# A norm's weights spread by two small matmuls, a first product group cut in two, and a scaling issued later

## The chip, the cores and the metric

The kernel runs on one core of a Trainium2 chip. A core has a matmul engine (TensorE, "PE" in the profile, with its weight loads as "PEld"), a vector engine (VectorE, "DVE"), a scalar engine (ScalarE, "ACT"), GpSimd ("POOL") and SyncE ("SP"), which here issues most of the transfers. The metric is the device time of one execution in microseconds (us); lower is better. Engines run side by side and wait for each other on semaphores. Each engine works through its own instructions in order.

## The reference, cut to what matters

One encoder layer over 2048 tokens of width 1024. Its first step, the only one that the change touches, is an RMS norm of the input and the first products with the mixer's input weights:

```python
def rmsnorm(x, gain):
    x32 = x.astype(jnp.float32)
    y = x32 * lax.rsqrt(jnp.mean(jnp.square(x32), axis=-1, keepdims=True) + EPS)
    return (y * gain.astype(jnp.float32)).astype(x.dtype)

def mlstm_mixer(xn, w_in, b_gates, head_norm, w_out):
    u = xn @ w_in                       # 1024 -> q 512, k 512, v 1024, o 1024, gates 16
    q, k, v, o, g = jnp.split(u, [...])
    ...                                 # forward and backward scan over 16 chunks of 128 tokens
    return h.astype(xn.dtype) @ w_out

h = x
xn = rmsnorm(h, norm_mix[0])
h = h + mlstm_mixer(xn, w_in, b_gates, head_norm, w_out)
h = h + sqrelu_mlp(rmsnorm(h, norm_mlp[0]), mlp_w1, mlp_w2)
...                                     # a gated embedding term and a last norm
```

## The kernel before, in words

All products are made from float32 numbers split into two parts: `hi`, the number rounded to TensorE's reduced float32, and `lo`, the rest. ACT casts the `hi`, DVE subtracts to get the `lo`, and three products (hi by hi, hi by lo, lo by hi) make one full product. So every operand costs a cast on ACT and a subtraction on DVE before PE can use it.

The first stage computes the first 512 columns of v for tokens 1024 to 2047 (block 1), in eight groups of 128 tokens (tiles). Its actors are:

- `p0` and `p1`, two `Prep` objects with four tiles of 128 tokens each. `p0` goes tile by tile, so that products can start early: `dma1(j)` loads tile j (`raw`, 512 KB); `norm1(j)` squares it on ACT (a sum along the row is a by-product), makes the inverse root by a chain of five small DVE and two small ACT operations (`rstd`), and scales it on DVE into `xs`, with the norm's weights as a row in all 128 partitions (`rowc["mix"]`); `tr1(j)` transposes the eight 128x128 blocks of `xs` on PE into two accumulator banks (`pt`), from which four casts on ACT and four subtractions on DVE fill `xT`. `p1` goes by all four tiles at once: `square(j)` four times, `scale()` (one `rstd` and four scalings on DVE), and `tr(k)` for the eight slices k, with the norm's weights per partition (`gains["mix"]`).
- `v0`, a job with four weights of 512 KB (`v0.weights`, each two slices of 128 rows) and eight groups (`v0g`). `prep()` of a weight is one cast on ACT (`whi`) and one subtraction on DVE (`wlo`). A group is 24 matmuls of 512 columns into one accumulator bank (`psv`) and a copy out (`ev`, on DVE for even tiles and on ACT for odd ones). Group 0 has an order of its own: first all 16 products with `whi`, then the 8 with `wlo`.

Three things set the order. Between `strict(V, A, TE)` (L1466) and `strict()` (L1504) the instructions of DVE, ACT and PE are issued on each engine in just the order in which the program text names them. Transfers of SP are issued in the order of the text as far as their buffers are free, and run in that order. After `strict()` the framework itself orders each engine's instructions by the order of the text and by the times that it expects; the last line of the stage, `v0.groups = [lambda: weave(...)]`, hands it tile 3's group together with `p1`'s eight `tr(k)`. Accumulator banks come from a pool of four for products (`ps_mm`) and one of three for transposes (`ps_tr`). In the profile most instructions carry L98 or L100, the lines of the helper that issues them, strict or not; so they are told apart by their tiles.

Of the kernel before, what the change touches and what calls it, by code (L numbers as in the profile page):

```python
# [8 lines left out]
F32 = mybir.dt.float32  # L9
F32R = mybir.dt.float32r  # L10
AF = mybir.ActivationFunctionType
ALU = mybir.AluOpType
# [4 lines left out]
P = 128  # L17
S = 2048
D = 1024
KD = D // P  # L20
# [15 lines left out]
def hybrid_mlstm_kernel(  # L36
# [23 lines left out]
    const = ctx.enter_context(tc.tile_pool(name="const", bufs=1))  # L60
# [4 lines left out]
    def ps_mm(name):  # L65
        return psm.tile([P, 512], F32, tag="mm", bufs=4, name=name)
# [7 lines left out]
    def Ht(name, shape, dt=F32):  # L74

        return sb.tile(shape, dt, tag="H", bufs=NH, name=name)
# [5 lines left out]
    def St(name, shape, dt=F32):  # L82

        return sb.tile(shape, dt, tag="S", bufs=6, name=name)
# [20 lines left out]
    def strict(*engines):  # L105
        for e in (V, A, TE):
            e.strict = e in engines

    V, A, G, TE, SP = Engine(nc.vector), Engine(nc.scalar), nc.gpsimd, Engine(nc.tensor), nc.sync


    rowc = {}
# [22 lines left out]
    ones = const.tile([P, P], F32, name="ones")  # L135
# [3 lines left out]
    def gain_load(nm, g):  # L139
        SP.dma_start(gains[nm], g.rearrange("(k p) -> p k", p=P))  # L140
# [15 lines left out]
    def weave(main, side):  # L156
        n, done = len(main), 0
        for i, f in enumerate(main):
            upto = -(-(i + 1) * len(side) // n)
            for g in side[done:upto]:  # L160
                g()
            done = upto
            f()
# [5 lines left out]
    def rstd(ss, n, out=None):  # L169

        T = lambda nm: sb.tile([P, 8], F32, tag=nm, bufs=3, name=nm)[:, :n]
        a, y, t = T("rsa"), T("rsy"), T("rst")
        V.tensor_scalar_add(a, ss, EPS)
        act(y, a, AF.Ln)
        act(y, y, AF.Exp, scale=-0.5)
        V.tensor_tensor(t, a, y, op=ALU.mult)
        V.tensor_tensor(t, t, y, op=ALU.mult)
        V.tensor_scalar(t, t, -0.5, 1.5, op0=ALU.mult, op1=ALU.add)
        out = y if out is None else out
        V.tensor_tensor(out, y, t, op=ALU.mult)  # L180
        return out

    def small(nm, bufs=3):
        return sb.tile([P, 8], F32, tag=nm, bufs=bufs, name=nm)

    def mm3(ps, lh, ll, rh, rl, first, last, **kw):
        TE.matmul(ps, lh, rh, start=first, stop=False, **kw)
        TE.matmul(ps, lh, rl, start=False, stop=False, **kw)
        TE.matmul(ps, ll, rh, start=False, stop=last, **kw)
# [63 lines left out]
    class Prep:  # L253
# [50 lines left out]
        def norm1(self, j):  # L304
            ss = small("ss1")
            xs = Ht("xs", [P, D])
            A.activation(xs, self.raw[j], AF.Square, scale=1.0 / 32.0, accum_out=ss[:, 0:1])
            r = rstd(ss[:, :1], 1)
            V.scalar_tensor_tensor(xs, self.raw[j], r[:, 0:1], rowc["mix"], op0=ALU.mult, op1=ALU.mult)
            self.xs1 = xs  # L310

        def tr1(self, j):
# [254 lines left out]
    def store(c, dst, src):  # L567
        (SP if c >= 8 else G).dma_start(dst, src)
# [39 lines left out]
    def v_groups(prs, blk, c0, n, ws, nk):  # L608

        gate = c0 + n == D  # L610

        def group(tt):
            def f():
                ps = ps_mm("psv")[:, :n + 16 * gate]
                pr = prs[tt // 4]
                sl = slice((tt % 4) * P, (tt % 4 + 1) * P)
                if blk == 1 and c0 == 0 and tt == 0:

                    for k in range(KD):
                        for xk in (pr.hi, pr.lo):  # L620
                            TE.matmul(ps, xk[k][:, sl], ws[k // nk].hi[:, k % nk], start=k == 0 and xk is pr.hi, stop=False)
                    for k in range(KD):
                        TE.matmul(ps, pr.hi[k][:, sl], ws[k // nk].lo[:, k % nk], start=False, stop=k == KD - 1)
                else:
                    for k in range(KD):
                        w = ws[k // nk]
                        mm3(ps, pr.hi[k][:, sl], pr.lo[k][:, sl], w.hi[:, k % nk], w.lo[:, k % nk],
                            k == 0, k == KD - 1)
                t = St("ev", [P, 512])[:, :n]
                (A.copy if tt % 2 else V.tensor_copy)(t, ps[:, :n])  # L630
                store(blk * 8, pr.rows(v_d, blk * 8 + tt)[..., c0:c0 + n], t)
                if gate:
                    if tt == 0:
                        gt[blk] = sb.tile([P, 8, 16], F32, tag="gt", name="gt")
                    V.tensor_copy(gt[blk][:, tt], ps[:, n:])
            return f
        return [group(tt) for tt in range(8)]

    def w_rows(k0, k1, c0, n):
        return w_in[k0 * P:k1 * P, c0:c0 + n].rearrange("(k p) n -> p k n", p=P)  # L640
# [1 line left out]
    def v_jobs(prs, blk):  # L642
        wa = [Weight(w_rows(k, k + 2, VC, 512), [P, 2, 512]) for k in range(0, KD, 2)]
        wb = [Weight(w_rows(k, k + 4, VC + 512, 256), [P, 4, 256]) for k in range(0, KD, 4)]
        wc = [Weight([w_rows(k, min(k + 3, KD), c0, n) for c0, n in ((VC + 768, 256), (GC, 16))],
                     [P, min(3, KD - k), 272]) for k in range(0, KD, 3)]
        b, c = v_groups(prs, blk, 512, 256, wb, 4), v_groups(prs, blk, 768, 256, wc, 3)
        return Job(v_groups(prs, blk, 0, 512, wa, 2), wa), Job(c + b, wc + wb)

    def gate_rows(blk):  # L650

        pt = ps_tr("ptg")[:, :P]
        TE.transpose(pt, gt[blk].rearrange("p c g -> p (c g)"), ident)
        t = sb.tile([P, P], F32, tag="gr", name="gr")
        V.tensor_copy(t, pt)
        for c in range(8):
            d = g_d[blk * 8:blk * 8 + 8]
            if blk == 1:
                SP.dma_start(d[c], t[c * 16:c * 16 + 16])
            else:  # L660
                q = c % 4
                SP.dma_start(d[c - q:c - q + 4, :, 32 * q:32 * q + 32].rearrange("c g t -> g c t"),
                             t[c * 16:c * 16 + 16].rearrange("g (c t) -> g c t", c=4))
# [776 lines left out]
    def x_tile(t):  # L1440
        return x[t * P:(t + 1) * P, :]

    pa = {1: [Prep(lambda j, s=s: x_tile(8 + s * 4 + j), gains["mix"]) for s in range(2)],
          0: [Early(lambda j, s=s: x_tile(s * 4 + j), gains["mix"], f"mix{s}_d") for s in range(2)]}
# [22 lines left out]
    v0 = jobs[1, "v"][0]  # L1467
    v0.ready = True
    p0 = pa[1][0]
    p0.dma1(0)  # L1470
    rowc["mix"] = Ht("row_mix", [P, D])
    SP.dma_start(rowc["mix"], norm_mix[0].partition_broadcast(P))
    v0.weights[0].dma()
    p0.dma1(1)
    for w in v0.weights[1:]:
# [1 line left out]
    p0.dma1(2)  # L1477
    p0.dma1(3)
    p0.norm1(0)
    v0.weights[0].prep()  # L1480
    p0.tr1(0)
    v0.weights[1].prep()
    v0.weights[2].prep()
    v0.weights[3].prep()
    p0.norm1(1)
    v0g = list(v0.groups)
    v0g[0]()
    p0.tr1(1)
    pa[1][1].dma()
    p0.norm1(2)  # L1490
    p1 = pa[1][1]
    p1.square(0)
    p1.square(1)
    v0g[1]()
    gain_load("mix", norm_mix[0])
    gain_load("hn", head_norm[0])
    p0.tr1(2)
    p0.norm1(3)
    p1.square(2)
    p1.square(3)  # L1500
    p1.scale()
    v0g[2]()
    p0.tr1(3)
    strict()  # L1504
    v0.groups = [lambda: weave(v0g[3:4], pa[1][1].steps()[2:])] + v0g[4:]
    pairs1[0].side.append(lambda: gate_rows(1))
    pairs1[1].side.append(gate_bias)

# [145 lines left out]
    n = ENTER[-1] + NQ  # L1654
# [34 lines left out]
    for t in range(NC):  # L1689
# [12 lines left out]
        g, i = t // 4 + 1, t % 4  # L1702
# [45 lines left out]
```

## Time and profile before

| | |
|---|---|
| Median of 3 runs | 2401.54 us (2399.94 to 2401.57) |
| Span of the profiled execution, first to last instruction | 2396.9 us (no time beside the span is listed for it) |
| PE busy | 2359.8 us, 98% |
| DVE, ACT, POOL busy | 65%, 49%, 26% |
| Mean granted PE clock | 0.997 |

The page lists for each engine its busy time, its share of the span and its number of instructions. "Windows" give the same for stretches of the span. The timeline lists instructions in order of time: start in us, duration in us, engine, line, operation, output <- inputs, shapes, count, and in brackets how long the engine stood idle before it and whom it waited for. The chain of work that ended last is followed back from the last instruction, at each step to what released it.

### The profile page before, as it was taken

How to read it: one execution, taken by the hardware profiler on the slowest of the kernel's cores; microseconds unless marked ns; L12 is line 12 of the kernel's file. 1: busy time of each engine (PE TensorE's matmuls, PEld its weight loads, DVE VectorE, ACT ScalarE, POOL GpSimd, SP SyncE). 2: the span in 40 equal slices, each digit the busy share in tenths (PEclk: the TensorE clock that was granted, in tenths of full speed). 3: DMA queues.
4: the chain of work that ended last, by engine and by line, in shares of the span. 5: the costliest groups of instructions: out<-in, count | busy, mean ns of one | idle time of the engine just before them, and what ended most of it. 6: DMA issues, size and time to landing. Idle time of an engine off the chain costs nothing.

```text
span 2396.9 us, 31578 instructions
## 1 busy us (share of the span) xinstructions
PE 2359.8 (98%) x11221; PEld 1949.9 (81%) x11221; DVE 1564.8 (65%) x2611; ACT 1164.3 (49%) x2166; POOL 629.9 (26%) x679
## 2 busy tenths in 40 slices
PE   7999999999999999999999999999999999999998
PEld 6988888788889887888888888787888888888886
DVE  6677545557778887666685544767666667666665
ACT  5234434437788874343353333444444444455554
POOL 0041122124333324446533332011111111111121
PEclk9999999999999999999999999999999999999999
DMA  5676656868668883456663332568686776796453
GB/s 177 228 225 196 192 144 224 281 220 295 230 227 296 277 269 110 132 169 209 215 228 106 106 114 71 176 134 196 142 189 164 170 170 153 173 216 178 136 138 87
DMA packets 274038, 441.18 MB, mean 184 GB/s; under 512 B 48936, under 2 KB 182440, under 8 KB 273880
## 3 DMA queue, kind: packets, MB, share of 16 engines
q1 hardware_dynamic: 211608, 309.00, 39.3%
q0 software_dynamic: 61984, 129.64, 23.2%
q8 instruction: 88, 1.44, 0.2%
q14 instruction: 70, 0.57, 0.1%
q10 hardware_dynamic: 288, 0.52, 0.1%
HBM read 263.39 MB, written 175.50 MB: 183 GB/s over the span
## 4 chain that ended last, share of the span: by engine, by line
PE 91%; DVE 4%; ACT 2%; issue 1%; DMA 1%; POOL 0%; DVEq 0%; ACTq 0%; SPq 0%; POOLq 0%
PE pa L100 33%; PE pb L100 16%; PE pc L100 8%; PE pg L100 7%; PE psf L100 7%; PE psv L100 7%; PE pso L100 5%; PE pn L100 2%; PE pl L100 2%; PE pu L100 2%; PE pt L100 1%; DVE op L100 1%; PE pS L100 0%; ACT jk L100 0%; DMA wst<-in_mlp_w 0%
## 5 line engine op out<-in xcount | busy, mean ns | idle before, releaser
L100 PE MATMUL pa<-op 128*128 128x512 f32 x3360 | 824.2, 394 | 3.6 <-ACT e L100 2.1
L100 PEld LDWEIGHTS pa<-op 128*128 128x128 f32 x3360 | 629.5, 188 | 155.7 <-ACT e L100 4.4
L100 PE MATMUL pb<-op 128*128 128x512 f32 x1632 | 407.7, 394 | 0.8 <-DVE op L100 0.8
L100 PEld LDWEIGHTS pb<-op 128*128 128x128 f32 x1632 | 306.2, 188 | 73.8 <-DVE op L100 1.1
L100 DVE TENSOR_TENSOR op<-sa,op 128x1024 fp32r<-128x1024 f32 (+2 forms) x176 | 189.1, 1080 | 143.3 <-ACT op L100 109.7
L100 ACT CAST op<-sa 128x1024 fp32r<-128x1024 f32 (+2 forms) x176 | 156.6, 894 | 189.7 <-PE pb L100 98.1
L1297 POOL DMA_DIRECT2D h_d<-o x96 | 94.8, 1033 | 529.9 <-DVE o L100 443.7
L100 ACT COPY e<-pa 128x512 f32<-128x512 f32 x160 | 93.7, 586 | 278.4 <-PE pa L100 277.9
L100 PE MATMUL pc<-op 128*128 128x512 f32 x768 | 191.9, 394 | 0.1
L100 PEld LDWEIGHTS pc<-op 128*128 128x128 f32 x768 | 144.1, 188 | 34.6 <-DVE op L100 0.6
L100 PE MATMUL psv<-whi,xT 128*128 128x272 f32 (+2 forms) x720 | 161.1, 317 | 0.6 <-DVE xT L98 0.6
L100 PE MATMUL psf<-xT,whi 128*128 128x512 f32 x512 | 160.9, 395 | 0.0
L100 ACT CAST op<-wst 128x512 fp32r<-128x512 f32 x112 | 92.5, 834 | 113.9 <-DVE op L100 59.8
L100 DVE TENSOR_TENSOR op<-wst,op 128x512 fp32r<-128x512 f32 x112 | 122.8, 1099 | 30.8 <-ACT op L100 18.5
L467 POOL TENSOR_TENSOR sa<-wst 128x512 f32<-128x512 f32 x32 | 58.8, 1838 | 262.2 <-PE pb L100 167.3
L100 PEld LDWEIGHTS psv<-whi,xT 128*128 128x128 f32 x720 | 118.6, 188 | 9.8 <-DVE xT L98 0.8
L100 PE MATMUL psv<-wlo,xT 128*128 128x272 f32 (+2 forms) x360 | 113.8, 316 | 0.0
L100 PEld LDWEIGHTS psf<-xT,whi 128*128 128x128 f32 x512 | 95.4, 188 | 21.3
L100 DVE TENSOR_TENSOR op<-hst,op 128x384 fp32r<-128x384 f32 (+1 forms) x96 | 65.5, 688 | 64.7 <-ACT op L100 45.1
L100 PE MATMUL pso<-whi,hThi 128*128 128x512 f32 x256 | 102.0, 399 | 2.6 <-ACT nt L100 1.4
L100 PE MATMUL pg<-whi,xTh 128*128 128x512 f32 x256 | 101.4, 397 | 0.0
L100 PE MATMUL psf<-xT,wlo 128*128 128x512 f32 x256 | 100.9, 394 | 0.0
(261 smaller groups left out, 4371.4 us busy)
## 6 DMA issues: line engine op xcount, KB each, us to landing
wst<-in_mlp_w SPq DMA_DIRECT2D x96, 512.0 KB, 5.2
h_d<-o POOLq DMA_DIRECT2D x96, 512.0 KB, 13.4
hid_d<-e SPq DMA_DIRECT2D x128, 256.0 KB, 2.5
hst<-hid_d SPq DMA_DIRECT2D x64, 384.0 KB, 6.8
wst<-in_mlstm_w_in SPq DMA_DIRECT2D x44, 512.0 KB, 5.2
vst<-v_d SPq DMA_DIRECT2D x31, 512.0 KB, 4.7
raw<-in_x SPq DMA_DIRECT2D x16, 512.0 KB, 6.6
kq<-kq_d SPq DMA_DIRECT2D x16, 512.0 KB, 4.0
```

The costliest lines, as they stand in the source:

```text
L100: r = f(*a, **kw)
L467: eng.tensor_tensor(s[:, 0], r1[:, :, P:], r2[:, :, P:], op=add_)
L1297: G.dma_start(rows(h1_d, 2 * q + i), o[i], accum_op=add_)
```

## The change

The norm's weights are loaded as one row of 4 KB (`row1`). Two matmuls with a row of ones spread its halves over 128 partitions in two accumulator banks. The scaling of tile 0 reads those banks in two halves; then ACT copies both halves into a tile in SBUF, which the later tiles use. Group 0 becomes two functions, `high` (16 products) and the rest (8 products and the copy out), with the transpositions of tile 1 between them. The norm of tile 1 goes ahead of the cast of the fourth weight. The scaling of `p1` goes behind the transpositions of tile 3.

```diff
             r = rstd(ss[:, :1], 1)
-            V.scalar_tensor_tensor(xs, self.raw[j], r[:, 0:1], rowc["mix"], op0=ALU.mult, op1=ALU.mult)
+            for g, sl in rowc["mix"]:
+                V.scalar_tensor_tensor(xs[:, sl], self.raw[j][:, sl], r[:, 0:1], g, op0=ALU.mult, op1=ALU.mult)
             self.xs1 = xs
...
         def group(tt):
+            first = blk == 1 and c0 == 0 and tt == 0
+            pr, sl = prs[tt // 4], slice((tt % 4) * P, (tt % 4 + 1) * P)
+            ps1 = []
+
+            def high():
+                ps = ps_mm("psv")[:, :n]
+                ps1.append(ps)
+                for k in range(KD):
+                    for xk in (pr.hi, pr.lo):
+                        TE.matmul(ps, xk[k][:, sl], ws[k // nk].hi[:, k % nk], start=k == 0 and xk is pr.hi, stop=False)
+
             def f():
-                ps = ps_mm("psv")[:, :n + 16 * gate]
-                pr = prs[tt // 4]
-                sl = slice((tt % 4) * P, (tt % 4 + 1) * P)
-                if blk == 1 and c0 == 0 and tt == 0:
-
-                    for k in range(KD):
-                        for xk in (pr.hi, pr.lo):
-                            TE.matmul(ps, xk[k][:, sl], ws[k // nk].hi[:, k % nk], start=k == 0 and xk is pr.hi, stop=False)
+                ps = ps1[0] if first else ps_mm("psv")[:, :n + 16 * gate]
+                if first:
                     for k in range(KD):
                         TE.matmul(ps, pr.hi[k][:, sl], ws[k // nk].lo[:, k % nk], start=False, stop=k == KD - 1)
...
-            return f
-        return [group(tt) for tt in range(8)]
+            return [high, f] if first else [f]
+        return [f for tt in range(8) for f in group(tt)]
...
     p0.dma1(0)
-    rowc["mix"] = Ht("row_mix", [P, D])
-    SP.dma_start(rowc["mix"], norm_mix[0].partition_broadcast(P))
+    row1 = const.tile([1, D], F32, name="row1")
+    SP.dma_start(row1, norm_mix[0].unsqueeze(0))
+    halves = [slice(n * 512, (n + 1) * 512) for n in range(2)]
+    rowc["mix"] = []
+    for sl in halves:
+        pb_ = ps_mm("prow")
+        TE.matmul(pb_, ones[0:1], row1[:, sl], start=True, stop=True)
+        rowc["mix"].append((pb_, sl))
     v0.weights[0].dma()
     p0.dma1(1)
...
     p0.norm1(0)
+    row = Ht("row_mix", [P, D])
+    for pb_, sl in rowc["mix"]:
+        A.copy(row[:, sl], pb_)
+    rowc["mix"] = [(row, slice(0, D))]
     v0.weights[0].prep()
     p0.tr1(0)
     v0.weights[1].prep()
     v0.weights[2].prep()
+    p0.norm1(1)
     v0.weights[3].prep()
-    p0.norm1(1)
     v0g = list(v0.groups)
     v0g[0]()
     p0.tr1(1)
     pa[1][1].dma()
+    v0g[1]()
     p0.norm1(2)
     p1 = pa[1][1]
     p1.square(0)
     p1.square(1)
-    v0g[1]()
+    v0g[2]()
     gain_load("mix", norm_mix[0])
     gain_load("hn", head_norm[0])
     p0.tr1(2)
     p0.norm1(3)
     p1.square(2)
     p1.square(3)
+    v0g[3]()
+    p0.tr1(3)
     p1.scale()
-    v0g[2]()
-    p0.tr1(3)
     strict()
-    v0.groups = [lambda: weave(v0g[3:4], pa[1][1].steps()[2:])] + v0g[4:]
+    v0.groups = [lambda: weave(v0g[4:5], pa[1][1].steps()[2:])] + v0g[5:]
```

## The prediction

> **What bounds the kernel now.** I read the page first: the span, the engines, the chain by engine.
>
> ```profile
> span 2396.9 us, 31578 instructions
> PE 2359.8 (98%) x11221; PEld 1949.9 (81%) x11221; DVE 1564.8 (65%) x2611; ACT 1164.3 (49%) x2166; POOL 629.9 (26%) x679
> PE 91%; DVE 4%; ACT 2%; issue 1%; DMA 1%; POOL 0%; DVEq 0%; ACTq 0%; SPq 0%; POOLq 0%
> ```
>
> The matmul engine (PE) is the bound; only its idle time can be won, 37.1 us in all. The windows by stage say where it lies, and the chain in order of time where the steady run begins.
>
> ```profile
> 0.00:8.60 8.60, 0.00 (x0) 0.00 (x0) 2.17 (x7) 3.41 (x6) 0.83 (x7) 1.00 0.72 252
> 8.60:20.10 11.50, 9.62 (x40) 7.09 (x40) 8.81 (x15) 6.53 (x13) 0.00 (x0) 1.00 1.04 401
> 33.60:45.20 11.60, 9.83 (x55) 7.55 (x56) 11.04 (x19) 6.36 (x12) 0.00 (x0) 1.00 0.25 75
> 45.20:2396.00 2350.80, 2326.95 (x11064) 1924.65 (x11062) 1534.54 (x2546) 1137.04 (x2110) 629.04 (x672) 1.00 0.63 184
> 20.13 5.82 PE psv L98 x24
> 45.11 69.85 PE psv L100 x483
> ```
>
> The second number is the stretch, the third PE's busy time. Before 45.1 us PE stands 8.6 us waiting for data, some 2 us around the first tile and nearly 2 us between 33.6 and 45.2. After 45.1 it runs on. So the change is worth what it moves two moments by: the start of tile 1's products (20.13, call it T1), and the stretch after 33.6. The page gives no time beside the span; the median, 2401.54, is 4.6 us above it, and I carry that 4.6 over.
>
> The timeline of the first tile, all engines, thinned:
>
> ```profile
> 1.28 0.41 SPq L1472 DMA_DIRECT2D row_mix<-in_norm_mix  x1
> 4.61 1.06 ACT L98 ACTIVATE xs<-raw 128x1024 f32<-128x1024 f32 x1 [2.52 <-DMA raw<-in_x]
> 6.21 0.20 ACT L98 ACTIVATE rsy<-rsy 128x1 f32<-128x1 f32 x1
> 7.21 1.28 DVE L98 SCALAR_TENSOR_TENSOR xs<-raw,rsy,row_mix 128x1024 f32<-128x1024 f32 x1
> 8.03 1.05 ACT L98 CAST whi<-wst 128x1024 fp32r<-128x1024 f32 x1 [1.61 <-DMA wst<-in_mlstm_w_in]
> 8.88 1.70 PE L98 MATMUL pt<-ident,xs 128*128 128x128 f32 x7
> 9.11 1.23 DVE L98 TENSOR_TENSOR wlo<-wst,whi 128x1024 fp32r<-128x1024 f32 x1 [0.61 <-ACT whi L98]
> 9.77 0.37 ACT L98 CAST xT<-pt 128x256 fp32r<-128x256 f32 x1 [0.69 <-PE pt L98]
> 10.24 2.00 PE L98 MATMUL psv<-whi,xT 128*128 128x512 f32 x4
> 10.25 0.42 DVE L98 TENSOR_TENSOR xT<-pt,xT 128x256 fp32r<-128x256 f32 x1
> 11.48 0.37 ACT L98 CAST xT<-pt 128x256 fp32r<-128x256 f32 x1 [0.21 <-DVE xT L98]
> 11.75 2.94 ACT L98 CAST whi<-wst 128x1024 fp32r<-128x1024 f32 x3
> 12.83 3.50 DVE L98 TENSOR_TENSOR wlo<-wst,whi 128x1024 fp32r<-128x1024 f32 x3 [0.52 <-ACT whi L98]
> 14.60 1.06 ACT L98 ACTIVATE xs<-raw 128x1024 f32<-128x1024 f32 x1
> 15.78 2.01 PE L98 MATMUL psv<-wlo,xT 128*128 128x512 f32 x8
> 16.24 0.15 DVE L98 TENSOR_SCALAR rsa<-ss 128x1 f32<-128x1 f32 x1
> 17.66 1.29 DVE L98 SCALAR_TENSOR_TENSOR xs<-raw,rsy,row_mix 128x1024 f32<-128x1024 f32 x1
> 19.01 1.09 PE L98 MATMUL pt<-ident,xs 128*128 128x128 f32 x8 [1.22 <-DVE xs L98]
> 25.77 1.03 PE L98 MATMUL pt<-ident,xs 128*128 128x128 f32 x8
> 25.97 0.59 ACT L98 COPY ev<-psv 128x512 f32<-128x512 f32 x1 [0.81 <-PE psv L98]
> 26.86 1.67 DVE L98 TENSOR_TENSOR xT<-pt,xT 128x256 fp32r<-128x256 f32 x4 [1.70 <-ACT xT L98]
> ```
>
> What the reader sees: PE is fed by a relay of casts on ACT and subtractions on DVE. Tile 0's low pass ends about 17.8, then PE waits 1.2 us for xs of tile 1 (17.66 + 1.29), transposes until 20.1, and starts T1.
>
> The second place:
>
> ```profile
> 31.90 0.17 DVE L98 TENSOR_SCALAR rsa<-ss 128x4 f32<-128x4 f32 x1
> 33.67 2.74 DVE L98 TENSOR_SCALAR xs<-raw,rsy 128x1024 f32<-128x1024 f32 x4 [0.34 <-DVE rsy L98]
> 33.95 0.40 PE L100 MATMUL psv<-wlo,xT 128*128 128x512 f32 x1
> 34.57 0.30 PE L100 MATMUL pt<-ident,xs 128*128 128x128 f32 x1 [0.22 <-DVE xs L98]
> 37.37 0.70 ACT L98 CAST xT<-pt 128x256 fp32r<-128x256 f32 x2 [3.38 <-DVE xT L98]
> 37.40 0.72 PE L100 MATMUL psv<-whi,xT 128*128 128x512 f32 x2 [0.60 <-DVE xT L98]
> 38.89 1.01 DVE L100 TENSOR_TENSOR wlo<-wst,whi 128x816 fp32r<-128x816 f32 x1 [0.35 <-ACT whi L100]
> 39.81 2.06 DVE L100 SCALAR_TENSOR_TENSOR xT<-pt,g_mix,xT 128x512 fp32r<-128x512 f32 x3
> ```
>
> The four scalings of the second half stand on DVE ahead of tile 3's subtractions, and PE, after two products of tile 3, has only four transposes to do until 37.40. ACT's cast waited 3.38 us for DVE although the two write different tiles: both read one accumulator bank.
>
> **The change part by part. Load and spreading.** One 512 KB load becomes 4 KB; SP still issues one transfer (0.41). At the 401 GB/s of the second window, everything queued behind comes 1.3 us sooner. I cost that at nothing: only the first weight was waited for (until 8.03), and ACT will be held longer than that by the copies below. Without those copies it would be worth up to 1.3.
>
> The two row matmuls run where PE is idle (until 8.6). No row shows one. Nearest are 128x512 products in the reduced type, 0.5 us cold (2.00 / 4; cold are the first ones after the start, at half the later rate), and float32 transposes, 1.70 / 7 = 0.243 per 128 columns, 0.97 per 512. I take the second, being the same type. The row arrives behind the first tile, 4.61 + 0.47 (the issue distance) = 5.1, so the halves stand ready at about 6.1 and 7.0, before DVE asks at 7.21. Upper end: the row lands no earlier than the weight behind it did, 8.03; then the second half stands at 10.0 and all below shifts by 2.1 us.
>
> The Trainium skill, FP8 and Floating Point Precision, section TensorE Precision Notes, has true float32 as four passes through the array; at the cold 0.5 that would be 2.0 us each, the second half at 9.1, and the sum 1.2 us higher. No run here shows it yet.
>
> **First scaling and copies.** DVE's 1.28 becomes two halves out of the accumulator, 0.69 each (2.06 / 3, the 128x512 form): 7.21 to 8.6. ACT's two copies, 0.59 each, read the same banks; going by the 3.38 wait each follows its half's scaling, so 8.6 + 0.5 puts the first weight cast at w = 9.1, 1.1 later than 8.03.
>
> The Trainium skill, PSUM — Partial Sum Buffer, section PSUM bank collisions raise a hardware error, says ACT and DVE must not touch one bank's same partitions together, readers included, and that the compiler adds an order. The trace agrees, by the 3.38 us. Without that rule the copies would start at 6.4 and the sum be about 1.6 lower.
>
> **Order of tile 0.** From w: the subtraction of tile 0 starts at w + 2.2 (10.25 - 8.03), behind the first weight's; the third and fourth casts follow the first and second subtractions, 0.42 apart, so the second weight cast starts at w + 3.4 (before: 3.7; PE was late then). The third follows 0.95 later; the square of tile 1, now ahead of the fourth, at w + 5.3. DVE does weight subtractions 1 and 2 from w + 4.5, 1.14 each, so rsa comes at w + 6.8, not with the square's end. From rsa to the transposes took 16.24 to 19.01 = 2.77: now w + 9.6. Meanwhile the fourth cast, queued behind two small ACT operations that wait for DVE, starts at w + 7.4 and ends at w + 8.4; PE finishes the high pass at w + 9.3, without a loss. Transposes 1.1, low pass 8 x 0.23 = 1.85 (2.01 less the tail; the 24 of tile 1 took 5.82, the same rate): T1 = w + 12.55 = 21.65. That is 1.5 us later than 20.13. The transpositions do sit between the passes, but xs of tile 1 is no earlier (18.6 against 18.95), because w moved, and the low pass now comes after it. DVE's fourth weight subtraction (done w + 10.6) and the casts of tile 1 are ready before T1. From T1 to tile 3 the work is the same, so 1.5 is carried.
>
> **The later scaling.** It frees 34.35 to 37.40 = 3.05, of which four transposes at 0.13 (1.03 / 8) are work: -2.5. What is late next: tile 3's transposes end at 33.6 + 1.5 = 35.1, its subtractions take 1.67, rsa to the last scaling took 31.90 to 36.41 = 4.5: the second half is ready at 41.35. Tile 3's 24 products run from 35.15 to 40.75; nine transposes whose inputs are ready can fill 1.2 us more. So from nothing to 0.6, and up to 1.6 if the next weight's subtraction (1.01) slips into that chain. I take +0.5. The following casts and subtractions, 0.69 per slice, are faster than PE's three products and four transposes (1.2).
>
> Sum: +1.5 - 2.5 + 0.5 = -0.5: span 2396.4, time 2401.0.
>
> **Rivals.** (a) The copies don't wait for DVE, or the part costs nothing for another reason: w = 7.55, T1 = 20.1, total -2.1: 2399.4. Against: the 3.38 wait. (b) PE falls to half rate in a hole. The cold rows show the price: eight transposes at 0.243 against 0.13 and four products at 0.5 against 0.23, 2.0 us. A new hole of 2 us opens before the fourth weight: 2403.0. For: products were cold until 12.2 after a start at 8.65. Against: holes of 0.6 and 1.2 changed nothing.
>
> The Trainium skill, TensorE: Matmul & The Clock Gate, section Part 1, has the clock halve after an idle window of about 3.4 us; 2 us is short of that. The cold 3.6 us at the start agree with it.
>
> (c) The changed order doesn't do what it says: past the hand-made order the framework orders by itself, and put four transposes after only two products of tile 3 (34.57). Should it do so again, PE stands from 35.6 to 41.35 and the remaining work, 7.8 us as between 37.4 and 45.2, ends at 49.2, 4.0 later: 2405.5. Against: the subtractions no longer stand behind the scaling, so the products are ready first.
>
> (d) Slower: a load in a later stage falls one place back in its queue.
>
> ```profile
> 879.32 9.16 DMA z<-x_d
> 890.00:900.00 10.00, 8.92 (x44) 7.13 (x42) 9.91 (x14) 5.79 (x10) 0.00 (x0) 1.00 0.79 238
> ```
>
> The chain passes through this load and PE already loses 1.1 us behind it: another 9.2 gives about 2410; it decides from 4.8 us of delay on. (e) The mirror: the order recovers 5 or 6 of the 23.9 us idle after 45.2: 2395.
>
> **How the numbers follow.** My forecast 0.55, (a) 0.18, (b) 0.07, (c) 0.08, (d) 0.05, (e) 0.07. A difference of 0.2%, 4.8 us, is about what a measurement of this kernel can tell from no change. (e) and a little of (a) are faster: 0.09; (d) and the end of (c) slower: 0.07; same 0.84. Range: low, (a) without the 0.5 is 2398.9, less the 1.6 us between runs, 2397; high, the late row 2401.0 + 2.1 and the last wait in full, 1.1, with (c) almost whole: 2405.
>
> **What would show it.** The first weight cast at 9.1 behind two copies that wait for DVE (right), or near 7.5 (a). The fourth cast near 16.5. T1 near 21.6. No stand of PE over 1 us between 35 and 42; a block of transposes waiting for xs there is (c). 128x512 products at 0.5 after 15 us are (b). The prediction is wrong if the row matmuls take over 1.4 us each, if xs of tile 1 comes well before 18, or if stretches after 50 us differ in more than a shift.

## The result, and the profile after

| | before | after |
|---|---|---|
| Median | 2402.11 us (2398.88 to 2409.52, 21 runs) | 2398.35 us (2396.22 to 2401.39, 21 runs) |
| Ratio after to before | | 0.9982, 95% interval 0.9976 to 0.9988 |
| Span of the trace | 2396.9 us | 2396.6 us |

The change makes the kernel 0.18% faster, 4.3 us by the ratio: just inside the 0.2% that the prediction called no change, and inside its range of 2397 to 2405. The two traces differ by 0.3 us only, so most of the gain isn't in them: the trace of before is one of its fastest executions. (The profiled run of after took 2398.35, 1.75 more than its span. By the same 1.75 the traced execution of before took about 2398.7, an estimate, less than any of the 21 runs; the 4.6 that the prediction carried over is mostly the distance from this fast execution to a median of others.)

The page of after, span and engines:

```profile
span 2396.6 us, 31587 instructions
...
PE 2364.5 (99%) x11225; PEld 1951.6 (81%) x11225; DVE 1565.9 (65%) x2612; ACT 1165.9 (49%) x2168; POOL 629.9 (26%) x679
```

The windows of after (stretch, its length, busy time of PE, PEld, DVE, ACT, POOL with counts, granted PE clock, DMA share, GB/s):

```profile
8.60:20.10 11.50, 10.14 (x30) 6.64 (x31) 8.62 (x15) 7.06 (x13) 0.00 (x0) 1.00 1.03 374
22.20:35.60 13.40, 13.30 (x66) 10.55 (x64) 7.12 (x20) 9.00 (x22) 0.00 (x0) 1.00 0.35 102
35.60:48.00 12.40, 12.40 (x69) 10.05 (x70) 11.11 (x22) 7.79 (x15) 0.00 (x0) 1.00 0.51 152
```

In the third stretch, which answers to 33.6 to 45.2 of before, PE has no idle time left. The timeline of after, thinned:

```profile
4.82 2.04 PE L100 MATMUL prow<-row,ones 1*128 1x512 f32 x2 [4.82 <-DMA row<-in_norm_mix]
...
6.65 1.91 PE L98 MATMUL prow<-row,ones 1*128 1x512 f32 x2
...
7.98 0.59 ACT L98 COPY row_mix<-prow 128x512 f32<-128x512 f32 x1 [1.64 <-DVE xs L98]
...
8.60 0.75 DVE L98 SCALAR_TENSOR_TENSOR xs<-raw,rsy,prow 128x512 f32<-128x512 f32 x1 [0.66 <-PE prow L98]
9.38 0.59 ACT L98 COPY row_mix<-prow 128x512 f32<-128x512 f32 x1 [0.82 <-DVE xs L98]
9.86 1.05 ACT L98 CAST whi<-wst 128x1024 fp32r<-128x1024 f32 x1
...
12.56 7.07 PE L98 MATMUL psv<-whi,xT 128*128 128x512 f32 x15 [0.53 <-DVE xT L98]
...
16.50 0.15 DVE L98 TENSOR_SCALAR rsa<-ss 128x1 f32<-128x1 f32 x1
...
17.02 1.03 ACT L98 CAST whi<-wst 128x1024 fp32r<-128x1024 f32 x1
...
17.92 1.28 DVE L98 SCALAR_TENSOR_TENSOR xs<-raw,rsy,row_mix 128x1024 f32<-128x1024 f32 x1
...
19.47 1.03 PE L98 MATMUL pt<-ident,xs 128*128 128x128 f32 x8
...
20.26 2.10 PE L98 MATMUL psv<-wlo,xT 128*128 128x512 f32 x8
...
22.20 0.40 PE L98 MATMUL psv<-whi,xT 128*128 128x512 f32 x1
...
38.67 2.74 DVE L98 TENSOR_SCALAR xs<-raw,rsy 128x1024 f32<-128x1024 f32 x4
...
39.63 0.49 PE L100 MATMUL pt<-ident,xs 128*128 128x128 f32 x3
...
41.33 1.00 DVE L100 TENSOR_TENSOR wlo<-wst,whi 128x816 fp32r<-128x816 f32 x1
```

The reader sees the relay start later (first weight cast at 9.86 instead of 8.03, behind two copies that wait for DVE), tile 1's products start at 22.20 instead of 20.13, and the transposes of the second half go between tile 3's products as their inputs come, three at a time.

To compare traces, two landmarks serve: T1, the start of tile 1's products, and the first product into the accumulator `pa`, which all kernels reach in the same way. Its row, before and after:

```profile
L100 PE MATMUL pa<-xT,op x96: 387/393/400, 114.8 to 254.0; 128*128 128x512 f32 x96
```

```profile
L100 PE MATMUL pa<-xT,op x96: 387/393/402, 113.9 to 253.0; 128*128 128x512 f32 x96
```

After is 0.9 us ahead at `pa` and gives 0.6 of it back on the way to the end (2282.7 against 2282.1 from there). These are the landmarks of all traces, read from the same rows; only the first two columns belong to the changed stage.

| kernel | T1 | T1 to `pa` | `pa` to the end |
|---|---|---|---|
| before, first trace | 20.13 | 94.7 | 2282.1 |
| before, second trace (e1) | 21.08 | 96.3 | 2282.0 |
| later scaling alone (e2) | 20.84 | 92.1 | 2283.1 |
| row alone (e3) | 21.51 | 94.2 | 2282.8 |
| cut group alone (e4) | 20.60 | 94.4 | 2282.5 |
| stand filled (e5) | 20.34 | 94.7 | 2281.9 |
| early products (e6) | 19.55 | 94.7 | 2285.1 |
| cut and scaling, no row (e7, e12) | 20.70, 20.48 | 91.8, 91.8 | 2281.0, 2280.8 |
| scaling and early products (e8) | 19.71 | 92.0 | 2284.3 |
| stand lengthened (e9) | 21.04 | 102.4 | 2285.1 |
| the same, filled (e10) | 20.09 | 100.0 | 2283.9 |
| after (first, e11) | 22.20, 21.85 | 91.7, 91.7 | 2282.7, 2283.3 |

In the ranges of runs below, three far outliers are left out (2574.71 us in the before of e5 to e8, 11154.0 in e6, 10220.74 in e8); the medians count them.

### The profile page after: what moved, and what is told of

Its sections match the earlier page's. It is cut to its first block, busy times and chain, and to the rows that moved or that the text cites. A ratio compares the mean times of both kernels' runs of the same rounds, so it can differ in the third digit from the quotient of the medians.

```text
span 2396.6 us, 31587 instructions
## 1 busy us (share of the span) xinstructions
PE 2364.5 (99%) x11225; PEld 1951.6 (81%) x11225; DVE 1565.9 (65%) x2612; ACT 1165.9 (49%) x2168; POOL 629.9 (26%) x679
## 4 chain that ended last, share of the span: by engine, by line
PE 59%; DVE 1%; issue 1%; DMA 0%; ACT 0%; POOL 0%; ACTq 0%; DVEq 0%; POOLq 0%
PE pa L100 29%; PE pb L100 14%; PE pg L100 7%; PE pc L100 7%; PE pl L100 2%; DVE op L100 0%; DMA wst<-in_mlp_w 0%; DVE raw L100 0%; DVE z L100 0%; DVE e L100 0%; ACT op L100 0%; PE pt L100 0%; ACT e L100 0%; DVE h L100 0%; POOL sa L474 0%
```

## The experiments

Two theories. A: the terms of the prediction, in every execution alike. B: executions of before differ in how long PE runs at half rate, and the change takes slow stretches away. Each kernel was timed against before in five rounds; the first four share their runs of before (median 2402.65, 33 runs), as do e5 to e8 (2400.99, 31 runs) and e9 to e12 (2401.62, 33 runs).

**e1: before, unchanged.**

> The kernel before, unchanged, as a control and for a second trace of it. The runs of before spread over 2398.9 to 2409.5 us and those of after over 2396.2 to 2401.4, while the two traces at hand differ by 1.0 us at 110 us and by 0.3 us in the span. Theory A (the terms of the prediction: the later scaling -2.5, the first tile +1.5 or more, in every execution alike): ratio 1.000, and a trace like the first, tile 1's products from 20.1. Theory B (the clock: executions of before differ in how long PE stays at half rate at the start, and this is what the change takes away): ratio 1.000 too, but the trace, if of a run above 2401, shows products 0.43 apart after 12.3 us and tile 1's products from 21 or later.

Median 2401.28 (2399.41 to 2405.79, 11 runs), ratio 0.9999 (0.9990 to 1.0008). Its trace is of a run of 2401.13. First the start and then the place of the stand, from the timeline of PE ("the stand" is here the time in which PE, between two products of tile 3, has only four transposes to do):

```profile
12.94 5.38 PE L98 MATMUL psv<-whi,xT 128*128 128x512 f32 x12 [0.56 <-ACT whi L98]
18.17 2.01 PE L98 MATMUL psv<-wlo,xT 128*128 128x512 f32 x8
...
21.08 0.50 PE L98 MATMUL psv<-whi,xT 128*128 128x512 f32 x1
...
38.36 1.07 PE L100 MATMUL psv<-whi,xT 128*128 128x512 f32 x2 [0.60 <-DVE xT L98]
39.23 0.63 PE L100 MATMUL psv<-wlo,xT 128*128 128x512 f32 x1
39.66 0.63 PE L100 MATMUL psv<-whi,xT 128*128 128x512 f32 x1
40.08 1.91 PE L100 MATMUL pt<-ident,xs 128*128 128x128 f32 x8
```

In the first trace of before, the first and the last of these rows are

```profile
12.85 3.09 PE L98 MATMUL psv<-whi,xT 128*128 128x512 f32 x12 [0.62 <-ACT whi L98]
...
38.42 1.04 PE L100 MATMUL pt<-ident,xs 128*128 128x128 f32 x8
```

The same twelve products that took 3.09 in the first trace took 5.38, and tile 1 started 0.95 later. And after the stand PE is slow a second time: eight transposes in 1.91 instead of 1.04. The windows of the same trace give the reason in the column after POOL, the granted clock:

```profile
34.90:38.30 3.40, 1.68 (x6) 0.55 (x4) 3.40 (x7) 0.04 (x1) 0.00 (x0) 1.00 0.06 17
38.40:41.80 3.40, 3.40 (x13) 2.90 (x14) 2.66 (x5) 2.63 (x5) 0.00 (x0) 0.52 0.74 228
```

After the stand the clock is at half for about 3.4 us, which puts 1.6 us on the way from T1 to `pa` (96.3 against 94.7). The first trace had the same stand without this. So one kernel has both, as theory B says; how often, two traces don't tell (the granted clock of every run does in part, behind e11). The Trainium skill, TensorE: Matmul & The Clock Gate, section Part 1, has a free-running window of 3413 ns over which PE's activity is judged, and half rate after an idle one; the 3.4 us of this half rate agree, and a stand of 3.05 us can fill such a window nearly or be split between two.

**e2: the later scaling alone.**

```diff
-    p1.scale()
     v0g[2]()
     p0.tr1(3)
+    p1.scale()
```

> Before, with only the scaling of the second half moved behind the transposes of tile 3. Theory A: the stand of PE between 34.3 and 37.4 goes, 2 to 2.5 us, and nothing is given back ahead of it: about 2399.7, ratio 0.9990, and the best of the three parts. Theory B: the same 2 to 2.5 us, with the spread of before kept (some runs over 2404), so the median stays above that of after.

Median 2397.87 (2395.85 to 2400.80, 11 runs), ratio 0.9978 (0.9969 to 0.9987): this part alone gives the whole gain. Its window over the place of the stand:

```profile
34.30:45.00 10.70, 10.67 (x59) 8.44 (x59) 9.65 (x20) 6.49 (x13) 0.00 (x0) 1.00 0.57 176
```

PE is busy 10.67 of 10.70. T1 to `pa` takes 92.1 instead of 94.7: 2.6 us, about theory A's size (2 to 2.5). The times say 5.3 with an interval of 3.1 to 7.4; the runs above 2401 are gone, so theory B's spread of before isn't kept. That surplus over 2.6 is what theory B has to explain.

**e3: the row alone.** The load, the two matmuls, the halves in the first scaling and the copies, as in the diff; order of tile 0 and scaling as before.

> Before, with only the weights' row loaded once, spread by the two matmuls and copied. Theory A: the first weight cast moves from 8.0 to 9.9 as in the trace of after, tile 1's products to about 21.5: +1.5 us, ratio 1.0006. Theory B: PE is busy from 4.8 us, leaves half rate at a steadier time, runs spread over 5 us at most instead of 10, and the median is 2 or more below that of before: ratio 0.999 or less.

Median 2401.95 (2400.05 to 2403.33, 11 runs), ratio 0.9998 (0.9989 to 1.0006). T1 at 21.51, as theory A had it: 0.4 to 1.4 us later than in the two traces of before. In the times this isn't seen, and neither is the gain that theory B gave it, though the runs lie within 3.3 us, as B said. The row is no help; PE, working on it from 4.8 us, was still at half rate in this trace until about 17 (15 products in 6.02 us from 12.55).

**e4: the cut group alone.** `high`, tile 1's transposes and the low pass, with tile 1's norm ahead of the fourth weight's cast; row and scaling as before.

> Before, with only the first group cut in two, tile 1's transposes between the passes and its norm ahead of the fourth weight's cast (row load and scaling as before). Theory A: without the copies the first weight cast stays at 8.0, so the whole order comes 1.9 us earlier than in after: xs of tile 1 done at 17.3, its transposes to 18.5, the low pass to 20.4: tile 1's products at about 20.3, +0.2 us: ratio 1.0001. Theory B: less waiting of PE between 12 and 19 us; if this steadies the clock, the spread shrinks and the ratio is 0.999 or less.

Median 2400.66 (2398.56 to 2402.09, 11 runs), ratio 0.9991 (0.9982 to 1.0000). T1 at 20.60, 0.3 later than theory A's 20.3. From its timeline:

```profile
16.47 1.29 DVE L98 SCALAR_TENSOR_TENSOR xs<-raw,rsy,row_mix 128x1024 f32<-128x1024 f32 x1
17.67 1.22 DVE L98 TENSOR_TENSOR wlo<-wst,whi 128x1024 fp32r<-128x1024 f32 x1
```

xs of tile 1 is done at 17.8, not 17.3: 1.2 earlier than in before, but the low pass then stands behind it. PE reached the full rate as early here as in the first trace of before (12.5 and 12.0), and against that trace the cut loses 0.5 at T1. The interval of the times reaches from a gain of 4 us to none, so a small gain isn't excluded.

**e5: the stand filled.** In before, after `p0.tr1(3)`:

```diff
+    pf = ps_s("fill")
+    for _ in range(12):
+        TE.matmul(pf, p0.hi[0][:, 0:P], v0.weights[0].hi[:, 0], start=True, stop=True)
```

> Before, with 12 products more (128x512, 2.8 us, results unused) placed on PE just where it stands behind the second half's scaling; the scaling keeps its place, and PE has nothing else to do there. Theory A (the stand itself is all that the later scaling wins): nothing to gain, the stand is only filled: ratio 1.000, runs as wide as before's (2398.7 to 2409.5). Theory B (in a part of the executions PE falls to half rate in this stand, as in the second trace of before, where products after 38.4 us lie 0.43 apart until 42): PE is busy throughout, no product is slow after 34 us, the runs above 2405 go and the median falls by 1 to 2 us: ratio 0.9993.

Median 2399.96 (2398.64 to 2401.52, 11 runs), ratio 0.9997 (0.9988 to 1.0006). T1 to `pa` 94.7: the stand is still paid in full, and nothing is slow behind it. The runs are narrower than those of before beside it (2398.26 to 2404.14, of which none is above 2405), but the interval holds 1: not settled by the times.

**e6: early products.** In before, ahead of the first norm:

```diff
+    pw = ps_s("warm")
+    for _ in range(20):
+        TE.matmul(pw[:, :P], ident, ident, start=True, stop=True)
```

> Before, with 20 float32 products of 128 columns (the identity by itself, results unused) on PE from about 1.5 us, while it waits for the first tile. Theory A: PE is not what the first tile waits for; ratio 1.000. Theory B: the first products run at full rate from about 8.6 instead of from 12.3 or 17.8 (the two traces of before), tile 1's products start at 20.1 in every execution instead of at 20.1 to 21.1; the stand at 34 us stays, so a part of the spread stays: median 0.5 to 1.5 us lower, ratio 0.9996.

Median 2401.83 (2399.74 to 2405.55, 11 runs), ratio 1.0005 (0.9996 to 1.0014): the gain that theory B gave it didn't come. The first half of theory B did. The 20 products show as 40 instructions. The timeline of PE:

```profile
2.12 5.50 PE L98 MATMUL warm<-ident 128*128 128x128 f32 x38
8.52 1.09 PE L98 MATMUL pt<-ident,xs 128*128 128x128 f32 x8 [0.89 <-DVE xs L98]
...
19.55 0.50 PE L98 MATMUL psv<-whi,xT 128*128 128x512 f32 x1
```

The eight transposes run at full rate from the start (1.09 us), and T1 is the earliest without a change of order. But the stage gained is lost later: from `pa` to the end this kernel takes 2285.1, 3.0 more than before. The place is between 906 and 2162 us, far from the edit; why isn't settled. Another order of PE's work is not the reason: behind `pa` PE loads its weights for the same tiles in the same order in all the traces.

**e7 and e12: cut and later scaling, the row loaded as before.** After without the row matmuls and copies.

> After, with the norm's weights loaded into all partitions as before: the cut group and the later scaling without the row matmuls and copies. Theory A: the first weight cast returns from 9.9 to 8.0, tile 1's products from 22.2 to 20.6 as in the trace with the cut alone: 1.6 us below after: 2396.8. Theory B: the same, and PE waits less between 12 and 19 us than in the kernel with the scaling alone, so the spread is the smallest so far. A rival to both, that early PE work in the row matmuls is what narrows the spread of after: runs as wide as those of before.

> The cut group and the later scaling with the weights loaded into all partitions as before, a second time, beside after. Both theories: the copies cost after 1.5 us on tile 1, so this one is 1.5 to 2 us below after and about 5 below before: 2396.4, ratio 0.9978. If the row matmuls have no net cost, it equals after.

Medians 2396.26 (2394.86 to 2399.43, 9 runs) and 2395.73 (2394.86 to 2398.23, 11 runs), ratios 0.9979 (0.9970 to 0.9989) and 0.9980 (0.9971 to 0.9989). Beside e12 ran after itself (e11). T1 is 1.4 us earlier than in after (20.48 against 21.85), from the timelines of PE, first this kernel, then after:

```profile
20.48 0.40 PE L98 MATMUL psv<-whi,xT 128*128 128x512 f32 x1
```

```profile
21.85 0.40 PE L98 MATMUL psv<-whi,xT 128*128 128x512 f32 x1
```

The medians beside each other differ by 2.5 us, though the intervals of the two ratios overlap. The traces differ by 3.7: 1.2 is there at `pa`, 2.5 comes later (2280.8 against 2283.3 from `pa`). Of this 2.5, about 1 lies near 440 us, where e12's lead over after's second trace grows from 1.5 to 2.4: all traces but e12's have PE at half rate for 3.4 us somewhere between 435 and 452 us (6.8 us in e10), in after for instance

```profile
438.70:442.11 3.41, 3.41 (x12) 2.89 (x11) 2.65 (x5) 0.67 (x1) 0.00 (x0) 0.50 0.73 227
```

and e12's has none. The remaining 1.5 isn't explained. This version's medians are the lowest of all: the row is the part of the change that costs. Against theory B, e7's spread of 4.6 us isn't the smallest (e5 has 2.9); against the rival, it is narrower than the 5.9 of before beside it.

**e8: later scaling and early products.**

> Before, with the later scaling and the 20 early products. Theory A: as the later scaling alone, 2397.9. Theory B: no half rate at the start, no stand at 34 us: tile 1's products at 20.1 always, 0.7 us below the trace with the later scaling alone (there they began at 20.84), and the narrowest runs: median 2397.2, all within 3 us.

Median 2397.41 (2396.07 to 2401.03, 11 runs), ratio 0.9984 (0.9975 to 0.9994). T1 at 19.71 and T1 to `pa` 92.0: the earliest `pa` of all, 111.7. The 2284.3 from there take it back, as in e6. The time lies between theory B's 2397.2 and theory A's 2397.9 and doesn't tell them apart; the runs, 5 us wide, are not the 3 of theory B.

**e9 and e10: the stand lengthened, and filled.** In before the four scalings are written three times (`for j in list(range(4)) * 3`); e10 has e5's products beside it, 34 of them.

> Before, with the four scalings of the second half written three times over (same result), so that PE's stand at 34 us is 5.5 us longer, about 8.5 us, in every execution. Theory A (only the stand counts): 5.5 us above before. Theory B (PE falls to half rate in a long stand): the fall now comes in every execution: products after the stand 0.43 apart for 3 to 5 us, 1.5 to 2.5 us on top of the 5.5, against an average of about 1 in before.

> The same long stand, filled on PE by 34 products with unused results (8 us). Theory A: the time of the long stand alone (e9), within 0.5 us. Theory B: 1.5 to 2.5 us below the long stand alone, and no product slower than 0.25 after the stand in the trace.

e9: median 2406.71 (2405.01 to 2410.34, 11 runs), ratio 1.0022 (1.0013 to 1.0031). e10: 2406.45 (2405.25 to 2407.09, 11 runs), ratio 1.0020 (1.0011 to 1.0029). Windows behind the stand, e9 and then e10:

```profile
43.60:48.70 5.10, 5.08 (x16) 4.24 (x17) 3.13 (x6) 1.63 (x4) 0.00 (x0) 0.50 0.13 51
```

```profile
42.60:48.00 5.40, 5.33 (x32) 4.48 (x33) 5.20 (x10) 3.55 (x7) 0.00 (x0) 1.00 0.13 49
```

In the traces theory B is seen at its plainest: the long stand is followed by 5 us at a clock of 0.50 (the half rate begins inside it, at 38.5), the filled one by full rate, and T1 to `pa` differs by 2.4 us (102.4 and 100.0). In the medians it isn't: 0.3 us apart, where B wanted 1.5 to 2.5. The trace of e9 is of its slowest run, five of its 11 runs are below e10's median, and behind `pa` e10 is 1.8 us slower than before and e9 3.0, so the pair is not clean. That the fall comes in every execution of e9 isn't shown; A's 5.5 fits its 5.1.

**e11: after, a second time.**

> After, unchanged, beside the next kernel and for a second trace. Both theories: 2398.3, ratio 0.9982. Theory B: no slow product after 35 us in this trace either, while the moment at which PE reaches the full rate may differ (18 us in the first).

Median 2398.19 (2395.89 to 2398.82, 11 runs), ratio 0.9985 (0.9976 to 0.9994). No slow product between 35 us and `pa` here either.

**The granted clock of the other traces and of every run.** In each trace the changes of the granted clock lie whole steps of 3.41 us apart, and where the steps begin differs from execution to execution. Half rate came where the stand fills a whole step or all but: in e1 the stand is 35.3 to 38.4 and a step 35.15 to 38.57, in e9 it is 35.3 to 43.6 and holds nearly two steps, 35.10 to 41.93. Where a step ends well inside the stand the clock stayed full: in the first trace of before at 35.84 in a stand from 34.35 to 37.40, in e3 at 37.51, in e4 at 36.43, in e6 at 35.14. The six traces with an unfilled stand agree on this.

Every timed run but those of before in the result also has its mean granted clock on record, to 0.001; over the span, 0.001 is worth 2.4 us of full rate (idle stretches count in this mean too). In the before of e1 to e4, 18 of 33 runs read 0.996 or less, with a median of 2403.40 against 2400.75 of the other 15; in e2 it is 1 run of 11. The averages there, 0.9964 and 0.9975, are about 2.7 us apart, an estimate that is as large as the surplus of e2. Of e9's runs 8 of 11 read 0.996 or less, of e10's and e5's none. So half rate in untraced runs goes with the stand, but not with it alone: e3 and e4, which have the stand, show 1 such run of 22, and beside e11 the averages of before and after, 0.9970 and 0.9973, differ by less than 1 us.

## Why the prediction was right or wrong

**The load and the row matmuls: mis-sized.** 0.97 us each was taken from the transposes; the row shows two instructions for each half, and the second half stood ready at 8.56 instead of 7.0: 1.83 for the first (4.82 to 6.65) and 1.91 for the second. That is over the 1.4 that the prediction named as a sign of being wrong. DVE waited 0.66 for it. That the row lands at about 5 held (4.82). The Trainium skill's four passes at the cold rate (FP8 and Floating Point Precision, section TensorE Precision Notes) gave 2.0 each; the trace agrees to 0.2.

**Copies: right.** Both wait for DVE (1.64 and 0.82) and hold the first weight cast to 9.86; predicted 9.1, the difference being the late second half. Rival (a) is excluded by these waits, and e7, which has no copies, shows about what it would have been worth.

**Order of tile 0: right in the times, in part by luck.** From the weight cast the steps came at +6.6 (rsa), +7.2 (fourth cast) and +9.6 (transposes) against +6.8, +7.4 and +9.6. T1 came at 22.20, predicted 21.65. But xs of tile 1 was done at 19.20 (17.92 + 1.28), and the transposes at 19.47 show no wait for it: they came straight behind the high pass, whose 15 products took 7.07 from 12.56, most of it at half rate. The prediction let PE end that pass without a loss; that both ends lie within 0.3 us is luck.

**The later scaling: right in the mechanism, the remainder too high.** The second half was ready at 41.4 (predicted 41.35) and PE filled the time: the nine transposes whose inputs were there went between the products, and the next weight's subtraction came behind the scaling. Of the +0.5 nothing appeared. From T1 to `pa` the gain is 3.0 in the traces of after against the first of before, where -2.5 + 0.5 was summed. Rival (c), the old order of transposes, did not come.

**The sum: -0.5 was right against the first trace (-0.9 at `pa`, -0.3 at the end), and not against the median (-3.8).** The step that failed is the one that took that trace for the kernel: it said of the 4.6 us between span and median "I carry that 4.6 over". T1 of before's own order is anywhere between 20.1 and 21.1: six traces with that order (before, e1, e2, e5, e9, e10) have 20.13, 21.08, 20.84, 20.34, 21.04 and 20.09, and the granted clock became full at 11.95, 18.09, 17.48, 16.82, 18.04 and 12.98, so a late full rate goes with a late T1. And the stand can be followed by half rate, 1.6 us more in e1. Against the second trace of before, after is 3.5 us ahead at `pa` and 2.8 in the span. Rival (b) had the mechanism and the wrong kernel: the price was worked out for a new hole in after, while the old stand, longer than any new hole, paid it in before.

**What stays open.** The traces account for 0.3 to 2.8 of the 3.8 us between the medians. Executions of before above 2402 us, about half of them beside after, were not traced, and neither filling the stand nor lengthening it separated A from B in the times. That the later scaling brings the gain is shown by e2, and that half rate follows a stand which fills a step is shown in traces. The mean clocks of the runs fit half rate as the rest of the gain in e2; beside e11 they cover less than 1 us, and there the rest stays open.

## What to carry to other kernels

A stand of the matmul engine can cost more than its length: the one of 3 us was followed by 3.4 us at half rate in one of two traces of the same kernel. Look in several traces and at the mean clock of all runs, and let work that is needed later not go ahead of what the engine waits for. Here a transfer that nobody waited for was not worth replacing: the two matmuls and two copies that saved a 512 KB load stood in the relay that sets the start. One trace is one execution: before a sum is made against it, see where its time lies among the runs.

## What the runs showed of the hardware that was not expected

- The same instructions reach the full matmul rate at different moments: in the two traces of before at 11.95 and 18.09 us after the start, with PE first used at 8.65 and 8.73. Two row matmuls from 4.8 us did not bring it forward (17.03 in e3, 18.86 and 17.23 in after); 20 short identity products from 1.5 us did (4.42 in e6, 6.62 in e8).
- The records of the granted clock begin with its first rise, so the windows read 1.00 in the first cold stretch, where products are 0.43 us apart, but 0.52 and 0.50 in the later ones. Before the first rise, only the spacing of the products tells.
- Behind the first rise, the granted clock changed only at whole steps of 3.41 us, and a stand of 3 us led to half rate or not by how the steps lay across it (e1 and the first trace of before).
- A float32 matmul of 128x512 from one row of one partition took 1.83 to 1.91 us at half rate, in two instructions, where a product in the reduced type took 0.43 to 0.5.
